# A list scheduler's picture of PSUM banks and of a cold TensorE, block norms applied behind the projection, and down sums of two hidden tiles

## The chip, the core and the metric

The kernel runs on one core of a Trainium2 chip. The metric is the device time of one execution in microseconds (us); the time before is the median of three runs, 3055.63 us (3053.68 to 3060.42). TensorE (PE) multiplies, VectorE (DVE), ScalarE (ACT) and GpSimd (POOL) do the rest, SyncE (SP) issues the DMAs.

## What is computed

One step of a hybrid decoder layer, for a prompt of 2048 tokens and eight single decode tokens that share the weights, in float32:

```python
y = parallel_mixer(rms_norm(x, norm_mix), ...)        # p = h @ w_in; a width-31 depthwise conv on a gated half,
x = x + y                                             # a gated DeltaNet of 4 heads on the other; then w_out
x = x + memory_attend(rms_norm(x, norm_mem_q), ...)   # 4 heads over 256 memory tokens
x = x + swiglu(rms_norm(x, norm_ffn), w_gate, w_up, w_down)   # 1024 -> 2816 -> 1024
y = rms_norm(x, norm_f)

def rms_norm(x, g, eps=1e-6):
    return x * rsqrt(mean(x * x, -1) + eps) * g
```

The outputs are the two y, the new convolution and DeltaNet states and the memory's keys and values.

## The kernel before

The prompt is cut into NB = 4 blocks of TB = 512 tokens; the features lie on the partitions, in KC = 8 tiles of 128. Float32 precision is reached by splitting every factor into a high and a low part and adding three products (`three`), so each product of a 128x128 tile is three matmuls (x3 in the rows). The split of x into the two parts is made by `split_ps`: ScalarE writes the high part, VectorE subtracts for the low one. Weights arrive as `raw` tiles and are split into NW = 6 tiles `w`, by ScalarE and then GpSimd or VectorE, for the first block that uses them; the FFN's split tiles are kept in DRAM (`sums`) and read from there by the later blocks.

Stages in the profiled run: to 860 us the mixer's projections for the pairs of blocks (0, 1) and (2, 3), products `hd` (q, k, v, z), `glua` and `glub` from the tiles `hT`, with the DeltaNet heads (`dn_front`, `dn_chain`: pk, pq, pqk, pu, pch, po) and the depthwise convolution on VectorE (`cacc`, 480 instructions) beside them; to 945 memory keys and values; to 1303 output projection (`rg`) and attention (`sc`) of blocks 0 and 1; the FFN of block 0 to 1680; then output and attention of block 2, FFN 1, the same of block 3, FFN 2 (with the eight decode columns) and FFN 3. An FFN has NF = 22 hidden tiles f; for each there are seven products fx, fy, fz of 12 matmuls of 256 columns, and the down sums `dn`, which are added to x (`x<-dn,x`).

`norm_in` (L1121) prepares blocks 1 to 3 in two passes over x: the first loads each of 8 tiles `xl`, squares it (`sqj`) and sums the squares, whose row factor goes through `pss`, `rs`, `dg` and `prs` (TensorE, VectorE, GpSimd) to `rsb`; the second loads `xl` again, multiplies it by gain and `rsb`, and splits it into `hT`. Block 0 already does it the other way: its `hT` carry only the gain, and `evac` (L1554) multiplies by `rsb` when a product leaves PSUM. `down` (L2675) sums GF = 4 hidden tiles in a PSUM bank before it adds to x: NG = 6 groups, the last of two; a group's eight output tiles are spread over the four following f.

PSUM has eight banks: three under the tag mm, three under s, one each under o and cv. Nothing is issued as written: each operation goes on a `Tape`, and `Tape.order` (L283) lists them anew. It runs a clock for each engine, takes from each engine's ready operations the one with the lowest key, and adds the estimated duration from `cost` (L176) and a latency. What an operation depends on is found by comparing boxes (`box`, L207), so that two uses of different parts of one PSUM bank are independent. The result is one fixed order for each engine. TensorE has one estimated price for each shape, whatever went before.

Of the kernel before, what the change touches and what calls it, by code (L numbers as in the profile page):

```python
# [14 lines left out]
P = 128  # L15
# [29 lines left out]

PAIRS = [(b, b + 1) for b in range(0, NB, 2)]
GF = 4
NG = -(-NF // GF)
# [11 lines left out]
HOLD = 2  # L60
RES = 5
# [85 lines left out]
class Tape:  # L147
# [28 lines left out]
    def cost(self, eng, op, args, kw, outs, ins):  # L176
# [16 lines left out]
        if eng == "act":  # L193
            ptr = len(ins) - 1
            return 0.834 * n + (50 if psum_in else 94) + 93 * ptr, False, SETS.get(kw.get("func"))
# [87 lines left out]
    def order(self):  # L283
# [49 lines left out]
        dma_at, port_at, table = 0.0, 0.0, None  # L333
# [15 lines left out]
        while len(done) < N:  # L349
# [18 lines left out]
            while av:  # L368
                k, n = heappop(av)
                new = [x for x in tiles[n] if x not in given]  # L370
# [7 lines left out]
                if stop is None:  # L378
                    if e == "dve" and self.ops[n][7][1] and port_at > t + 150 and not skipped:

                        other = [(k2, m) for k2, m in av if not self.ops[m][7][1] and all(x in given for x in tiles[m])]
# [45 lines left out]
            done.append(n)  # L427
            lat = self.LAT["dma" if e == "sp" else e]
# [144 lines left out]
def hybrid_step(ctx: ExitStack, tc: tile.TileContext, i: dict, o: list):  # L573
# [209 lines left out]
    def span_of(k, left):  # L783

        n = KC // min(GF, left)
        return range(k * n, (k + 1) * n)

    def group(g):
        return range(GF * g, min(GF * (g + 1), NF))

    def down_keys(g, ms=range(KC)):

        return [("w_down", "f", KC * g + (m if g < NG - 1 else m // 2), 0) for m in ms if g < NG - 1 or m % 2 == 0]

    def ffn_steps(b):
# [3 lines left out]
        for f in range(NF):  # L799
            if f and not early:  # L800
                steps.append(("Q1", f))
            g = f // GF - 1
            ms = span_of(f % GF, NF - GF * (g + 1))
            if g < 0 or g >= NG - hold:
                g = None
# [7 lines left out]
            if g is not None:  # L813
                steps.append(("down", g, ms[0]))
            steps.append(("P4", f))
            if g is not None:
                steps += [("down", g, m) for m in ms[1:]]
        if not hold and b != NB - 1:
            steps += [("down", NG - 1, m) for m in range(KC)]
# [11 lines left out]
    def ffn_plan(b):  # L831
        at = {}
        for st, f, *j in ffn_steps(b):
            if st == "down":
                plan.extend(down_keys(f, j))
# [30 lines left out]
    for b in range(NB):  # L866
# [4 lines left out]
        elif b + 1 < NB:  # L871
            for g in range(NG - HOLD, NG):
                plan.extend(down_keys(g))
    plan.extend(down_keys(NG - 1))
# [3 lines left out]
    class WS:  # L878
# [28 lines left out]
        def load(self):  # L907
# [9 lines left out]
            else:  # L917
                w, kind, a, b_ = what
                src = wsrc[w]
                if kind == "c":  # L920
                    dma(r, src[a, b_], fr)
                elif kind == "f":
                    dma(r, src[a], fr)
# [197 lines left out]
    def norm_in(b, res, go=1):  # L1121

        acc = None
        yield go
        for second in range(2):
            xs = []
            for k in range(KC):
                while len(xs) < min(k + 3, KC):
                    yield ("t2", 1 + RES)
                    xs.append(t2("xl"))  # L1130
                    dma(xs[-1], xT[len(xs) - 1, :, cols_of(b)])
                x = xs[k]
                yield x
                if second:
                    yield ("act", 1)
                    a = act("hT")
                    V.scalar_tensor_tensor(out=x, in0=x, scalar=vcol("norm_mix", k), in1=rsb, op0=ALU.mult, op1=ALU.mult)
                    split_ps(x, a[:, 0, :TB], a[:, 1, :TB])
                    drop(x)
                    res[k] = a  # L1140
                else:
                    yield ("t2", 1 + RES)
                    j = square(x)
                    drop(x)
                    if acc is None:
                        acc = j
                    else:
                        G.tensor_tensor(out=acc, in0=acc, in1=j, op=ALU.add)
                        drop(j)
                yield 1  # L1150
            if not second:
                rs = yield from rstd([acc], TB)
                rsb = yield from spread(rs, TB)
        drop(rsb)
        res["rsb"] = None
# [278 lines left out]
    def scalars(b, hT, res):  # L1434
# [8 lines left out]
        if hT["rsb"] is None:  # L1443
            A.activation(out=bdf, in_=pb_, func=AF.Copy)
        else:
            V.tensor_tensor(out=bdf, in0=pb_, in1=hT["rsb"][:16], op=ALU.mult)
# [107 lines left out]
    def evac(out, pts, hT, func=AF.Copy):  # L1554
# [3 lines left out]
        for pt, lo, hi in pts:  # L1558
            if hT["rsb"] is None:
                A.activation(out=out[:, lo:hi], in_=pt, func=func)  # L1560
                continue
# [77 lines left out]
    def dn_front(h, b, sc, prev, out):  # L1639
# [27 lines left out]
        for c in range(NT):  # L1667
            j = small("chj", [P, DK], dt=mybir.dt.bfloat16, bufs=1)
# [10 lines left out]
        for c in range(NT):  # L1679
            j = small("chj", [P, DK], dt=mybir.dt.bfloat16, bufs=1)  # L1680
# [30 lines left out]
        yield lambda: not inverting  # L1711
        inverting.append(1)
# [21 lines left out]
        inverting.pop()  # L1734
# [44 lines left out]
    def dn_chain(h, b, f, sc, prev, out):  # L1779
# [8 lines left out]
        for c in range(NT):  # L1788
# [21 lines left out]
            j = small("chj", [P, DK], dt=mybir.dt.bfloat16, bufs=1)  # L1810
# [56 lines left out]
    kv_done, act_keep, fronts, inverting = [], [0], [], []  # L1867
# [157 lines left out]
    def glub_then(k):  # L2025
        def then(b, pts, dp):
# [5 lines left out]
            if hTs[b]["rsb"] is not None:  # L2032
                G.tensor_tensor(out=sg, in0=sg, in1=hTs[b]["rsb"], op=ALU.mult)
# [21 lines left out]
    for pair in PAIRS:  # L2055
# [58 lines left out]
        for b in pair:  # L2114
            S.until(lambda: "beta" in scs_[b], "scalars")
            if hTs[b]["rsb"] is not None:
                drop(hTs[b]["rsb"])
# [478 lines left out]
    def ffn(b, op, go_on):  # L2596
# [76 lines left out]
        dwt = {}  # L2673

        def down(g, m):  # L2675
            fs = group(g)
            S.until(lambda: all(f in hact for f in fs), "ff")
            for key in down_keys(g, (m,)):
                dwt[0] = [ws.get(*key)]
            spans = [(0, w), (w, 2 * w)] if b == DEC_F else [(0, TB)]  # L2680
            pts = [pm("dn", (P, hi - lo)) for lo, hi in spans]
            for n_, f in enumerate(fs):
                at = n_ if g < NG - 1 else 2 * (m % 2) + n_
                three(pts, wk(dwt[0], 0, at), wk(dwt[0], 1, at), hact[f], spans, n_ == 0, n_ == len(fs) - 1)
                tick()
            if g < NG - 1 or m % 2:
                ws.free(1)
            if b == DEC_F:
                add_half(m, pts)
            else:  # L2690
                add_x(xs, m, [(pts[0], 0, TB)], None)
            if g == NG - 1:
                fin.add(m)
            if m == KC - 1:
                drop(*[hact.pop(f) for f in fs])

        def rest():
            for g in range(NG - HOLD, NG):
                for m in range(KC):
                    down(g, m)  # L2700
# [3 lines left out]
        def last():  # L2704
            fs = (NF - 2, NF - 1)
            S.until(lambda: all(f in hact for f in fs), "ff")
            wts = [ws.get(*key) for key in down_keys(NG - 1)]
# [83 lines left out]
def lay_out(inp):  # L2791
# [33 lines left out]
    full = NF // GF * GF  # L2825
    wd = inp["w_down"][0].reshape(NF, P, KC, P)
    main = wd[:full].reshape(NG - 1, GF, P, KC, P).transpose(0, 3, 2, 1, 4).reshape(-1, P, TB)
    end = wd[full:].reshape(2, P, KC // 2, 2, P).transpose(2, 1, 3, 0, 4).reshape(-1, P, TB)
    out["w_down"] = np.concatenate([main, end])
# [35 lines left out]
```

## Time and profile before

| | |
|---|---|
| median of three runs | 3055.63 us |
| profiled execution | 3056.0 us |
| its span | 3054.3 us |
| granted TensorE clock, mean | 0.988 |
| PE busy | 2958.2 us (97%) |
| DVE busy | 1971.5 us (65%) |
| POOL busy | 1380.7 us (45%) |
| ACT busy | 1325.6 us (43%) |

All instructions carry the line of one helper (L450, L469 in the changed kernel), so they are told apart by their tiles: `pss<-ones,sqj` writes pss and reads ones and sqj. [...]

### The profile page before, as it was taken

To read this page: it belongs to the slowest core of one execution; us is meant where nothing else is said; L and a number is where in the kernel's file an instruction comes from. 1 tells how busy PE (TensorE), PEld (TensorE's weight loads), DVE (VectorE), ACT (ScalarE), POOL (GpSimd) and SP (SyncE) were. 2 spreads that over 40 slices of the span, in tenths; PEclk is the share of its full clock that TensorE was granted. 3 is DMA by queue.
4 is the path that set the end of the run, shared out by engine and by line. 5 is a ranking of instruction groups with operands and counts; after the bars stand their busy time and mean duration, and the time that the engine had idled before them with its cause. 6 is when DMAs were issued, how large, how long until landed. Compare 5 with 4: busy or idle time off the path is not lost.

```text
span 3054.3 us, 52803 instructions
## 1 busy us (share of the span) xinstructions
PE 2958.2 (97%) x18950; PEld 2625.0 (86%) x18950; DVE 1971.5 (65%) x3946; ACT 1325.6 (43%) x2695; POOL 1380.7 (45%) x1228
## 2 busy tenths in 40 slices
PE   8999989999999999989999999999999999999998
PEld 6898867888888878789988779988878999999997
DVE  7857888888986876687678885423576333553334
ACT  6643337543565343545455354333444332433333
POOL 3433333432446455678877204355512443444444
PEclk9999989999999999999999999999999999999999
DMA  6443334543676442277667748766534766676663
GB/s 232 153 131 101 116 114 142 160 147 96 189 255 188 134 140 80 89 245 265 233 251 262 238 136 283 253 227 232 180 117 145 241 215 218 207 244 221 220 221 109
DMA packets 358631, 567.24 MB, mean 186 GB/s; under 512 B 56832, under 2 KB 155072, under 8 KB 358352
## 3 DMA queue, kind: packets, MB, share of 16 engines
q1 hardware_dynamic: 358368, 563.86, 55.9%
q8 instruction: 150, 2.46, 0.3%
q14 instruction: 113, 0.93, 0.1%
HBM read 455.68 MB, written 108.64 MB: 185 GB/s over the span
## 4 chain that ended last, share of the span: by engine, by line
PE 72%; DVE 7%; DMA 4%; ACT 1%; issue 1%; POOL 1%; SPq 0%; POOLq 0%; DVEq 0%; ACTq 0%
PE dn L450 16%; PE fy L450 12%; PE rg L450 9%; PE fz L450 8%; PE fx L450 8%; PE sc L450 5%; PE hd L450 4%; DVE cacc L450 2%; PE pu L450 2%; PE glub L450 1%; PE glua L450 1%; DVE bit L450 1%; PE pch L450 1%; DMA Tm<-zt 1%; DMA w<-sums 1%
## 5 line engine op out<-in xcount | busy, mean ns | idle before, releaser
L450 POOL TENSOR_TENSOR w<-raw,w 128x512 fp32r<-128x512 f32 x683 | 931.4, 1369 | 955.0 <-ACT w L450 866.7
L450 ACT ACTIVATE w<-raw 128x512 fp32r<-128x512 f32 x912 | 568.3, 631 | 942.9 <-PE dn L450 231.9
L450 PE MATMUL dn<-ff,w 128*128 128x512 f32 (+2 forms) x2688 | 518.2, 346 | 0.8 <-ACT ffs L450 0.8
L450 PEld LDWEIGHTS dn<-ff,w 128*128 128x128 f32 x2688 | 421.5, 188 | 58.8 <-ACT ffs L450 1.0
L450 PE MATMUL fy<-op,w 128*128 128x256 f32 (+1 forms) x3168 | 426.8, 283 | 0.5 <-DMA w<-sums 0.5
L450 PEld LDWEIGHTS fy<-op,w 128*128 128x128 f32 x3168 | 403.0, 189 | 8.5 <-issue 1.4
L450 PE MATMUL hd<-hT,w 128*128 128x512 f32 (+2 forms) x1920 | 399.6, 359 | 8.8 <-ACT w L450 6.6
L450 DVE SCALAR_TENSOR_TENSOR cacc<-cu,cw,cacc 128x512 f32<-128x512 f32 x480 | 358.7, 747 | 16.2 <-ACT cacc L450 11.0
L450 PEld LDWEIGHTS hd<-hT,w 128*128 128x128 f32 x1920 | 306.4, 191 | 52.6 <-ACT w L450 6.8
L450 PE MATMUL fz<-op,w 128*128 128x256 f32 (+1 forms) x2112 | 286.4, 282 | 4.2 <-DMA w<-sums 2.1
L450 PE MATMUL fx<-op,w 128*128 128x256 f32 (+1 forms) x2112 | 285.7, 283 | 2.9 <-DVE op L450 1.6
L450 PEld LDWEIGHTS fx<-op,w 128*128 128x128 f32 x2112 | 270.9, 189 | 12.8 <-DVE op L450 2.1
L450 PEld LDWEIGHTS fz<-op,w 128*128 128x128 f32 x2112 | 265.9, 189 | 8.9 <-issue 3.9
L450 DVE TENSOR_TENSOR w<-raw,w 128x512 fp32r<-128x512 f32 x229 | 217.8, 959 | 69.6 <-ACT w L450 67.3
L450 DVE TENSOR_TENSOR x<-dn,x 128x512 f32<-128x512 f32 (+1 forms) x248 | 139.8, 567 | 174.9 <-PE dn L450 172.5
L450 POOL TENSOR_TENSOR sqj<-sqj,sqj 128x512 f32<-128x512 f32 (+1 forms) x98 | 130.2, 1328 | 266.9 <-ACT sqj L450 264.7
L450 PE MATMUL sc<-w,hT 128*128 128x512 f32 x768 | 193.2, 404 | 3.0 <-DVE w L450 1.8
L450 PE MATMUL rg<-catS,w 128*128 128x512 f32 (+2 forms) x960 | 191.9, 355 | 1.9 <-DVE x L450 1.9
L450 PE MATMUL rg<-pT,w 128*128 128x512 f32 x768 | 190.6, 399 | 0.3
L450 PEld LDWEIGHTS rg<-catS,w 128*128 128x128 f32 x960 | 153.9, 189 | 26.9 <-DVE x L450 2.2
L450 PEld LDWEIGHTS sc<-w,hT 128*128 128x128 f32 x768 | 142.7, 191 | 37.6 <-ACT pr L450 3.1
L450 PEld LDWEIGHTS rg<-pT,w 128*128 128x128 f32 x768 | 141.4, 188 | 33.6 <-ACT pr L450 3.0
(381 smaller groups left out, 4036.3 us busy)
## 6 DMA issues: line engine op xcount, KB each, us to landing
w<-sums SPq DMA_DIRECT2D x264, 512.0 KB, 4.4
raw<-in_w_gate_dram SPq DMA_DIRECT2D x176, 256.0 KB, 3.4
sums<-w SPq DMA_DIRECT2D x88, 512.0 KB, 3.2
raw<-in_w_down_dram SPq DMA_DIRECT2D x176, 256.0 KB, 3.4
raw<-in_w_up_dram SPq DMA_DIRECT2D x110, 256.0 KB, 2.7
raw<-in_w_in_dram SPq DMA_DIRECT2D x96, 256.0 KB, 2.8
raw<-in_w_out_dram SPq DMA_DIRECT2D x64, 256.0 KB, 3.2
raw<-wk SPq DMA_DIRECT2D x64, 256.0 KB, 2.6
```

The source lines that it names most:

```text
L450: fn(*args, **kw)
```

## The change

1. The planner: a PSUM tile has one box, so a bank is one piece in the dependencies. `bank_at` also keeps an engine off a bank until another engine's last access to it is over. TensorE's estimates count 1.9 times for 3.4 us after it has had a pause of over 1.8 us. A ScalarE instruction that also accumulates costs 92 ns more.
2. `norm_in` makes `hT` and the squares in one pass, with the gain only; `rsb` is applied in `evac` for every block. That takes away 24 loads of `xl` and 24 VectorE scalings, and ScalarE's direct evacuations of blocks 1 to 3; VectorE gets those evacuations: `raw<-hd,rsb` of 512 columns 12 to 36 and of 256 columns 0 to 24, zs and sg each 4 to 12 and 0 to 8; GpSimd gets `sg<-sg,rsb` 4 to 16. In all VectorE has 4280 instructions for 3946, GpSimd 1245 for 1228, SP's DMAs are 1842 for 1866, and TensorE's matmuls stay the same in number.
3. Down groups of two: NG = 11, HOLD = 3. At an even f from 2 to 18 all eight output tiles of group f/2 - 1 are done one behind the other (four weight tiles of two outputs each), at an odd f none but at the last. `x<-dn,x` of 512 columns go from 136 to 256, of 256 columns from 112 to 192; matmuls and weight tiles stay the same in number.
4. The DeltaNet inversions no longer wait for each other (`inverting` is gone), and the junk tile `chj` of the squared norms has four buffers for one.

```diff
 def box(self, a):
+        if a.name in self.psum:
+            return 0, 0, 0, 0
...
+        def bank_at(n, e):
+
+            return max([bank[x][1] + self.LAT[bank[x][0]][e] for x in banks[n] if x in bank and bank[x][0] != e], default=0.0)
...
                 k, n = heappop(av)
+                at_ = bank_at(n, e)
+                if at_ > t:
+                    ready[n] = at_
+                    push(n)
+                    n = None
+                    continue
...
+            if e == "pe" and s > clock[e] + 1800 and s > 5000:
+                slow = s + 3400
+            if e == "pe" and s < slow:
+                ns *= 1.9
...
     def norm_in(b, res, go=1):
...
+        for k in range(KC):
+            while len(xs) < min(k + 4, KC):
+                yield ("t2", 1 + RES)
+                xs.append(t2("xl"))
+                dma(xs[-1], xT[len(xs) - 1, :, cols_of(b)])
+            x = xs[k]
+            yield x
+            yield ("act", 1)
+            a = act("hT")
+            split_ps(x, a[:, 0, :TB], a[:, 1, :TB], scale=vcol("norm_mix", k))
+            res[k] = a
...
+        res["rs"] = yield from rstd([acc], TB)
+        res["rsb"] = yield from spread(res["rs"], TB)
...
         for pt, lo, hi in pts:
-            if hT["rsb"] is None:
-                A.activation(out=out[:, lo:hi], in_=pt, func=func)
-                continue
             V.tensor_tensor(out=out[:, lo:hi], in0=pt, in1=hT["rsb"][:, lo:hi], op=ALU.mult)
...
-            g = f // GF - 1
-            ms = span_of(f % GF, NF - GF * (g + 1))
-            if g < 0 or g >= NG - hold:
+            g = NG - 2 if f == NF - 1 else f // 2 - 1 if f % 2 == 0 and 0 < f < NF - 2 else None
+            if g is not None and g >= NG - hold:
                 g = None
...
-            j = small("chj", [P, DK], dt=mybir.dt.bfloat16, bufs=1)
+            j = small("chj", [P, DK], dt=mybir.dt.bfloat16, bufs=4)
...
-        yield lambda: not inverting
-        inverting.append(1)
```

The order that comes out differs at many places. Three of them, all on TensorE:

At the start, before: what stands between block 0's first products and the first product of block 1 (hd_304, hd_305, in the 256 and 264 columns that block 1 and the decode tokens make); prs spreads a row factor, pbd is the small product for beta and decay.

```order
L450 MATMUL prs_279<-dg_273,ones 128x512
L450 MATMUL pbd_329<-hT_235,wbd 16x512 x2
L450 MATMUL pbd_329<-hT_237,wbd 16x512
L450 MATMUL pbd_280<-wbd,hd_mix 8x16
L450 MATMUL pbd_329<-hT_237,wbd 16x512
L450 MATMUL pbd_329<-hT_239,wbd 16x512 x2
L450 MATMUL pbd_329<-hT_241,wbd 16x512 x2
L450 MATMUL pbd_280<-wbd,hd_mix 8x16 x15
L450 MATMUL pss_275<-ones,sqj_251 128x1 x4
L450 MATMUL pbt_333<-ident,bdf_330 128x16 x4
L450 MATMUL prs_287<-dg_281,ones 128x512
L450 MATMUL hd_304<-hT_291,w_219 128x256
```

After, from the same dnb (the decode tokens' norm) on; block 1's first product is now hd_295:

```order
L469 MATMUL dnb_286<-tbd_278,ones 128x8
L469 MATMUL hd_295<-hT_252,w_219 128x256 x3
L469 MATMUL hd_295<-hT_255,w_219 128x256
L469 MATMUL pbd_321<-hT_225,wbd 16x512 x2
L469 MATMUL pbd_321<-hT_227,wbd 16x512 x2
L469 MATMUL hd_295<-hT_255,w_219 128x256 x2
L469 MATMUL hd_295<-hT_258,w_219 128x256
L469 MATMUL pbd_321<-hT_229,wbd 16x512 x2
L469 MATMUL pbd_321<-hT_231,wbd 16x512 x2
L469 MATMUL pbd_321<-hT_235,wbd 16x512 x2
L469 MATMUL hd_295<-hT_258,w_219 128x256 x2
L469 MATMUL hd_295<-hT_261,w_219 128x256
```

Block 1's product moved from behind both prs to the row behind dnb; the first prs, prs_287, now stands four rows further down.

Near 404 us, before: chain work of block 1, block 3's row factor (prs_1019), and then block 3's first product (hd_985<-hT_1028):

```order
L450 MATMUL peb_1099<-dtmp_962,ones 128x64
L450 MATMUL pch_1020<-chr_1021,W_872 128x128
L450 MATMUL lnb_1022<-tbd_1013,ones 128x8
L450 MATMUL prs_1019<-dg_1014,ones 128x512
L450 MATMUL po_989<-chv_1033,at_724 128x128
L450 MATMUL pch_1020<-chv_1033,kd_722 128x128
L450 MATMUL pbd_1101<-hT_904,wbd 16x512 x2
L450 MATMUL pbd_1101<-hT_906,wbd 16x512 x2
L450 MATMUL pbd_1101<-hT_912,wbd 16x512 x2
L450 MATMUL pbd_1101<-hT_916,wbd 16x512 x2
L450 MATMUL pbd_1101<-hT_924,wbd 16x512
L450 MATMUL hd_985<-hT_1028,w_928 128x512
```

After: block 2's last product of the three (hd_974), block 3's first (hd_980) right behind it, with chain work between its parts:

```order
L469 MATMUL hd_974<-hT_882,w_918 128x512 x3
L469 MATMUL hd_974<-hT_929,w_918 128x512 x3
L469 MATMUL hd_974<-hT_931,w_918 128x512 x3
L469 MATMUL hd_980<-hT_965,w_885 128x512 x3
L469 MATMUL pm_981<-cd_927,ones 128x8 x4
L469 MATMUL hd_980<-hT_970,w_885 128x512 x3
L469 MATMUL po_960<-S_121,rb_716 128x128
L469 MATMUL po_960<-chv_975,at_719 128x128
L469 MATMUL pch_962<-chv_975,kd_717 128x128
L469 MATMUL hd_980<-hT_977,w_885 128x512 x3
L469 MATMUL lnc_994<-ones,cd_770_967 8x1 x4
L469 MATMUL pch_998<-S_983,kT_711 128x128
```

Block 3's product moved ahead of its row factor; hd_980, hd_1029 and hd_1039, 24 rows' worth of x3, stand ahead of prs_1026 but for the last x3.

Near 1750 us, before: attention scores sc of block 2 with the transposes psc of the decode tokens' scores scs between them:

```order
L450 MATMUL sc_3738<-w_3760,hT_3744 128x512 x3
L450 MATMUL sc_3739<-w_3760,hT_3744 128x512 x3
L450 MATMUL sc_3740<-w_3760,hT_3744 128x512 x3
L450 MATMUL sc_3754<-w_3760,hT_3744 128x512 x3
L450 MATMUL psc_3799<-ident,scs_3546 32x128
L450 MATMUL sc_3805<-w_3765,hT_3692 128x512 x3
L450 MATMUL sc_3805<-w_3770,hT_3694 128x512
L450 MATMUL psc_3799<-ident,scs_3546 32x128
L450 MATMUL sc_3805<-w_3770,hT_3694 128x512 x2
L450 MATMUL sc_3805<-w_3775,hT_3696 128x512 x2
L450 MATMUL sc_3796<-w_3765,hT_3692 128x512 x3
```

After: the last score products, the first products behind them, and psc:

```order
L469 MATMUL sc_3813<-w_3817,hT_3750 128x512 x3
L469 MATMUL sc_3814<-w_3817,hT_3750 128x512 x3
L469 MATMUL rg_3839<-pT_3819,w_3821 128x512 x3
L469 MATMUL rg_3848<-pT_3819,w_3821 128x512 x3
L469 MATMUL rg_3846<-pT_3819,w_3821 128x512 x3
L469 MATMUL rg_3839<-pT_3823,w_3829 128x512 x2
L469 MATMUL rg_3847<-pT_3819,w_3821 128x512 x3
L469 MATMUL rg_3839<-pT_3823,w_3829 128x512
L469 MATMUL rg_3846<-pT_3823,w_3829 128x512 x3
L469 MATMUL rg_3847<-pT_3823,w_3829 128x512 x3
L469 MATMUL rg_3848<-pT_3823,w_3829 128x512 x3
L469 MATMUL psc_3855<-ident,scs_3565 32x128 x2
```

Both psc moved from the beginning of the second group of scores to behind that group and the first rg.

## Rows read from the trace of the kernel before

**Rows 1.** The page's part 1: busy us, share of the span, instructions.
```profile
PE 2958.2 (97%) x18950; PEld 2625.0 (86%) x18950; DVE 1971.5 (65%) x3946; ACT 1325.6 (43%) x2695; POOL 1380.7 (45%) x1228
```

**Rows 2.** Windows: stretch, length, busy us (instructions) by engine, clock, DMA.
```profile
core 0: us, PE busy (x) PEld busy (x) DVE busy (x) ACT busy (x) POOL busy (x), PEclk, DMA share, GB/s
450.00:850.00 400.00, 391.15 (x2149) 322.77 (x2150) 346.96 (x790) 202.06 (x437) 155.94 (x184) 1.00 0.48 147
28.00:46.00 18.00, 11.42 (x58) 6.48 (x57) 12.84 (x38) 5.42 (x9) 8.36 (x11) 0.78 0.90 310
404.00:428.00 24.00, 17.39 (x74) 12.90 (x73) 17.74 (x45) 8.03 (x16) 7.07 (x12) 0.57 0.39 122
1743.00:1765.00 22.00, 16.08 (x59) 11.92 (x58) 18.31 (x48) 9.55 (x25) 0.00 (x0) 0.77 0.43 134
1350.00:1700.00 350.00, 348.14 (x2296) 314.64 (x2295) 261.64 (x341) 170.29 (x314) 269.36 (x188) 1.00 0.72 254
1850.00:1900.00 50.00, 50.00 (x387) 47.80 (x386) 25.56 (x42) 19.08 (x36) 20.59 (x14) 1.00 0.84 289
2700.00:2750.00 50.00, 48.90 (x396) 47.68 (x397) 25.48 (x43) 17.12 (x34) 21.45 (x15) 1.00 0.87 305
```

**Rows 3.** Timeline of TensorE at the start: start, length, instruction, [idle before, releaser].
```profile
31.76 2.07 PE L450 MATMUL prs<-dg,ones 128*128 128x512 f32 x2 [2.43 <-DVE dg L450]
...
39.30 0.39 PE L450 MATMUL pbt<-ident,bdf 16*128 16x16 f32 x4 [1.84 <-DVE bdf L450]
...
43.12 1.24 PE L450 MATMUL hd<-hT,w 128*128 128x256 f32 x4 [2.19 <-ACT hT L450]
```

**Rows 4.** Timeline of TensorE from 404 to 428.
```profile
414.96 1.87 PE L450 MATMUL pss<-ones,sqj 128*128 128x1 f32 x8 [2.75 <-POOL sqj L450]
...
421.57 2.04 PE L450 MATMUL prs<-dg,ones 128*128 128x512 f32 x2 [1.10 <-DVE dg L450]
...
427.74 0.62 PE L450 MATMUL hd<-hT,w 128*128 128x512 f32 x2
```

**Rows 5.** Timeline of TensorE from 1745 to 1762.
```profile
1744.67 3.88 PE L450 MATMUL sc<-w,hT 128*128 128x512 f32 x16
...
1753.74 0.39 PE L450 MATMUL psc<-ident,scs 128*32 128x128 f32 x1 [4.09 <-DVE scs L450]
...
1757.25 4.94 PE L450 MATMUL sc<-w,hT 128*128 128x512 f32 x11 [1.84 <-DVE w L450]
```

**Rows 6.** Waits of TensorE over the span: us, times, longest.
```profile
PE pu L450 <- DMA Tm<-zt: 6.6, 6, 2.5
...
PE pq L450 <- ACT chj L450: 5.2, 6, 1.8
...
PE pod L450 <- ACT chj L450: 3.2, 2, 1.7
...
PE ppt L450 <- ACT chj L450: 2.3, 1, 2.3
```

**Rows 7.** Groups of instructions, shapes apart: count | busy us, mean ns | idle before.
```profile
L450 DVE SCALAR_TENSOR_TENSOR cacc<-cu,cw,cacc 128x512 f32<-128x512 f32 x480 | 358.7, 747 | 16.2 <-ACT cacc L450 11.0
L450 DVE TENSOR_TENSOR w<-raw,w 128x512 fp32r<-128x512 f32 x229 | 217.8, 959 | 69.6 <-ACT w L450 67.3 <-DMA raw<-in_w_up_dram 0.5 <-DMA raw<-in_w_out_dram 0.4
L450 DVE TENSOR_TENSOR x<-dn,x 128x512 f32<-128x512 f32 x136 | 93.7, 689 | 128.9 <-PE dn L450 128.1
L450 DVE TENSOR_TENSOR x<-dn,x 128x256 f32<-128x256 f32 x112 | 46.1, 419 | 46.0 <-PE dn L450 44.3
L450 DVE SCALAR_TENSOR_TENSOR xl<-xl,vcol,rsb 128x512 f32<-128x512 f32 x24 | 17.0, 740 | 2.0 <-DMA xl<-in_xT_dram 1.1 <-ACT rsb L450 0.9
...
L450 DVE TENSOR_TENSOR raw<-hd,rsb 128x512 f32<-128x512 f32 x12 | 8.1, 684 | 3.2 <-ACT rsb L450 2.0 <-PE hd L450 1.2
...
L450 POOL TENSOR_TENSOR sg<-sg,rsb 128x512 f32<-128x512 f32 x4 | 5.2, 1291 | 14.1 <-ACT sg L450 14.1
```

**Rows 8.** Timeline of TensorE in FFN 3.
```profile
2717.95 0.59 PE L450 MATMUL fz<-op,w 128*128 128x256 f32 x3 [1.10 <-DMA w<-sums]
```

More of the change, by code (lines that the diff above doesn't have):

```diff
@@ L58 @@
 DEC_F = 2
-HOLD = 2
+HOLD = 3
 RES = 5
@@ L332, in order @@
         clock = dict.fromkeys(engines, 0.0)
-        dma_at, port_at, table = 0.0, 0.0, None
+        dma_at, port_at, table, slow = 0.0, 0.0, None, 0.0
+        banks = [[x for x in ts if x in self.psum] for ts in tiles]
+        bank = {}
+        def bank_at(n, e):
+            return max([bank[x][1] + self.LAT[bank[x][0]][e] for x in banks[n] if x in bank and bank[x][0] != e], default=0.0)
         start, end, ends = [0.0] * N, [0.0] * N, {}
@@ L379, in order @@
                     if e == "dve" and self.ops[n][7][1] and port_at > t + 150 and not skipped:
-                        other = [(k2, m) for k2, m in av if not self.ops[m][7][1] and all(x in given for x in tiles[m])]
+                        other = [(k2, m) for k2, m in av if not self.ops[m][7][1] and all(x in given for x in tiles[m]) and bank_at(m, e) <= t]
                         if other:
@@ L427, in order @@
             done.append(n)
+            for x in banks[n]:
+                bank[x] = e, max(fin, bank[x][1]) if x in bank and bank[x][0] == e else fin
             lat = self.LAT["dma" if e == "sp" else e]
@@ L1121, in norm_in @@
     def norm_in(b, res, go=1):
+        xs = []
         acc = None
         yield go
[L1125 to L1155, printed above, removed]
+        for k in range(KC):
[9 more added lines that the diff above has]
+            res[k] = a
+            yield ("t2", 1 + RES)
+            j = square(x)
+            drop(x)
+            if acc is None:
+                acc = j
+            else:
+                G.tensor_tensor(out=acc, in0=acc, in1=j, op=ALU.add)
+                drop(j)
+            yield 1
+        res["rs"] = yield from rstd([acc], TB)
+        res["rsb"] = yield from spread(res["rs"], TB)
     def norm_mem(res):
@@ L1442, in scalars @@
         bdf = t2("bdf", (16, TB))
-        if hT["rsb"] is None:
-            A.activation(out=bdf, in_=pb_, func=AF.Copy)
-        else:
-            V.tensor_tensor(out=bdf, in0=pb_, in1=hT["rsb"][:16], op=ALU.mult)
+        V.tensor_tensor(out=bdf, in0=pb_, in1=hT["rsb"][:16], op=ALU.mult)
         yield bdf
@@ L2031, in then @@
             evac(sg, pts, hTs[b], AF.Sigmoid)
-            if hTs[b]["rsb"] is not None:
-                G.tensor_tensor(out=sg, in0=sg, in1=hTs[b]["rsb"], op=ALU.mult)
+            G.tensor_tensor(out=sg, in0=sg, in1=hTs[b]["rsb"], op=ALU.mult)
         return then
@@ L2115, in hybrid_step @@
             S.until(lambda: "beta" in scs_[b], "scalars")
-            if hTs[b]["rsb"] is not None:
-                drop(hTs[b]["rsb"])
+            drop(hTs[b]["rsb"])
     dma(o[3], halo)
@@ L2698, in rest @@
             for g in range(NG - HOLD, NG):
-                for m in range(KC):
-                    down(g, m)
+                for j in range(KC // 2):
+                    down(g, j)
             if b == DEC_F:
```

83 lines of the change are left out of this document (33 added, 50 removed).

## Prediction

> **What bounds the kernel now.** I read the page's busy times first, then the windows, the waits of TensorE, the timeline of the stretches that stood out, and last the groups of instructions. TensorE is busy for 2958.2 of 3054.3 us [rows 1], 97%, so this kernel can gain only what TensorE loses: some 96 us of idle time, and the time in which its clock is granted at the lower of its two levels. VectorE (65%), GpSimd and ScalarE (under half) are not bounds on the mean. The windows say where the loss is [rows 2]. 50 us of FFN products (1850 to 1900) have no idle time at a granted clock of 1.00, and the whole FFN of block 0 (1350 to 1700) lacks 1.9 of 350 us. The mixer between 450 and 850 lacks 8.9 of 400, with VectorE busy for 347 of the 400. Three short stretches lose far more for their length: 28 to 46, 404 to 428 and 1743 to 1765, with clocks of 0.78, 0.57 and 0.77. [...]
>
> **The change, part by part.** The sum is made against the profiled execution, 3056.0 us, which is 0.4 us above the median of the three runs, 3055.63.
>
> A, the start. Before, block 1's input is loaded twice: first for the squares, then, once its norm is known, for the scaled copies from which the products are made. TensorE therefore waits for the norm, 2.43 us at 31.76 (dg), then 1.84 at 39.30 and 2.19 at 43.12, where block 1's first product at last begins [rows 3]. Now the copies are made from the raw input on its first pass, and the row factor is applied when a product leaves PSUM. The order puts block 1's first product right behind the dnb that ends block 0's, with pbd, prs and the other small products between its parts, instead of behind prs. Bound: idle 6.6 + 0.22 x 18 = 4.0, so 10.5 us. I take 9: the work that fills the stretch (12 matmuls of 256 and 12 of 264 columns, some 3 us, before the second half of the copies) does not quite cover the 5 us of waits for dg, so something stays. Low end 6.
>
> B, block 3's norm at 404. TensorE waits 2.75 us for the sum of squares at 414.96, 1.10 for dg at 421.57, and the first product of block 3 stands at 427.74 [rows 4]; in between it does fragments of the chain at half clock. In the new order block 3's first product, its second and all but the last of its third (8 + 8 + 7 groups of x3) stand ahead of prs: 69 matmuls of 512 columns. At 0.233 us apart (16 such matmuls of sc take 3.88 us of which the last is 0.39 [rows 5]: 3.49/15) that is 16.1 us of dense work where there were fragments. Bound: idle 6.6 + 0.43 x 24 = 10.3, so 16.9 us. I take 14. Low end 8: the three products fill the three banks of their tag and hold them until block 3's row factor is there, so a norm that is late moves the wait behind the third product.
>
> C, the decode scores at 1743. The two transposes psc wait 4.09 us for VectorE's scs, and the next scores 1.84 for w, which VectorE makes behind it [rows 5]. Now both psc stand behind all scores of the pair and behind the first rg products. Bound: 5.9 idle + 0.23 x 22 = 5.1, so 11 us. I take 7, the waits and 1 of the clock; low end 3, if another VectorE operand is late next.
>
> D, banks. "Waits for chj" are TensorE waiting for a bank that ScalarE still reads (a square, then an accumulator read): pq 5.2 us, pod 3.2, ppt 2.3 [rows 6], and five smaller ones of 0.6 to 1.0, 14.4 us in all. The planner before thought a part of the bank free at once. Now it knows the bank is one piece and that the accumulator costs more, so it puts other work there. I take half, 7, with 0 and 12 as ends. The six waits of pu for the Tm transfer (6.6 us) are not touched by banks; letting several inversions run at once moves them by 2 either way, so nothing.
>
> E, VectorE in the mixer. Blocks 1 to 3 lose 24 scalings of xl (740 ns), and gain 24 raw of 512 columns (684), 24 raw of 256 (taken as 419, the half-size x<-dn), and for zs and sg together 16 of either size. That is 24 x 0.684 + 24 x 0.419 + 16 x 0.685 + 16 x 0.419 - 24 x 0.740 = 16.4 + 10.1 + 11.0 + 6.7 - 17.8 = +26 us, with bdf and the STT form of hT +3: about 30 us [rows 7]. Against it the order moves depthwise taps (cacc, 747 ns) out of this part: 313 instead of 360 of the 480 stand ahead of the first attention-output add, -35 us. The net is -5 us, on an engine that is 87% busy in 450 to 850 while TensorE loses 8.9 us. But the new operations stand between a product and its bank, the taps did not. I take a loss of 2, between a gain of 4 and a loss of 8 (8.9 us of idle time nearly doubled).
>
> F, FFN of block 0. Down groups of two instead of four mean 11 instead of 6 sums for each of the 8 column tiles of a block. In block 0 that is some 24 more adds x<-dn at 689 ns, 17 us, and the taps that were moved (438 instead of 470 done at the first ffu) another 24; with the last chain step VectorE gets 55 us more in this stage. It had 88 us spare (350 - 262). TensorE lost 1.9 us there; with the spare down to 33 I scale by 88/33 to 5, a loss of 3, and take 5 with the three-bank tag turning over twice as often. Ends: a gain of 2 (all that is lost there) and a loss of 15 (the slices after 1600, in which VectorE has already least to spare, overflow).
>
> G, FFN of blocks 1 to 3. There VectorE is at half load and the extra adds cost nothing. What is new is the run of weights: 13 products with no down sum between them, then eight sums in a row on four tiles. Product-only stretches exist before: 1850 to 1900 has 50.00 of 50 at 289 GB/s, 2700 to 2750 48.90 with one wait of 1.10 us for a weight tile at 2717.95 [rows 2, 8]. I take 2, two such waits more; ends 0 and 10.
>
> Sum: 9 + 14 + 7 + 7 - 2 - 5 - 2 = 28 us, so 3056.0 - 28 = **3028 us**.
>
> [...] The rows show a VectorE add with one PSUM operand at 689 ns in the mean, and the split w<-raw,w of the same size, with two SBUF operands, at 959 [rows 7]. [...]
>
> **The rivals.**
> 1. Weight tiles come late in the long runs, and it ends slower. There are 10 such runs in a block, 40 in all. At the one wait that the trace shows, 1.10 us each, that is 44 us in place of G's 2: 3028 - 2 + 44 = 3070 us. It decides from (28 + 2)/40 = 0.75 us a run. For it: 2717.95 is exactly such a wait, and the four tiles of a group are now wanted one behind the other. Against it: 1850 to 1900 is longer than a run and has no wait. Chance 0.11.
> 2. The gaps only move. The order is fixed on the planner's estimates; the three banks hold block 3's products until its row factor comes, and other chain steps wait in front of them in the queue. If A, B and C bring half (15), D nothing, and the losses stay (9), it is -6: 3050 us, at the edge of what can be told from no change. That the planner's new rules don't do what they say belongs here: the chj waits then stay at 14. Chance 0.15.
> 3. VectorE becomes the bound in block 0's FFN and in the mixer: F 15, E 8, G 2 against 37: 3044 us. For it: VectorE's load there goes from 262 to about 317 of 350, unevenly. Against it: adds wait for TensorE now, for the most part, and can slide. Chance 0.09.
> 4. All goes well: 10.5 + 16.9 + 11 + 12 with no losses is 50: 3006 us. Chance 0.07.
> 5. The clock. The 50 us of products in 1850 to 1900 change banks every 12 matmuls of 256 columns and hold 1.00 [rows 2]; the new down sums change them every 6 of 512, which takes as long. If instead the clock fell in them as far as in 28 to 46 (0.78), about 490 us of down matmuls (2112, in units of 512 columns, at 0.233) would take 490 x (1/0.78 - 1) = 138 us more, 3166 us. [...] Chance 0.01.
>
> **How the numbers follow.** The forecast (3012 to 3044) has 0.57, the rivals 0.11, 0.15, 0.09, 0.07 and 0.01. 0.2% of 3055.6 is 6 us, about what a measurement of this kernel can tell from no change. Faster by more: the forecast, rivals 3 and 4 and a third of rival 2, 0.78. The same: most of the rest of rival 2 and the milder half of rival 1, 0.10. Slower: the rest, 0.12. Best ends together (4) give 3006; the low end of the range is there. At the top, the low ends of A to D (6 + 8 + 3 + 0 = 17) less the losses' upper ends (8 + 15 + 10 = 33) are +16, not all likely together; 3060 leaves most of rival 1 and rival 5 out, near 0.12, and a little below the low end.
>
> **What would show it.** Right: 28 to 46 and 404 to 428 with TensorE dense and the clock at 1.00; no psc wait near 1750; chj waits near 7 us; VectorE about 300 of 350 in block 0's FFN with TensorE idle there under 10 us. Wrong: waits of fx, fy, fz or dn for w<-sums that add up to over 20 us (rival 1); waits of products for raw<-hd,rsb or for rsb in the mixer (rival 2); waits of FFN products for x<-dn, or a longer FFN of block 0 (rival 3); lower clock in the down runs (rival 5).

## The result and the profile after

The changed kernel takes 3013.76 us (median of four runs, 3007.98 to 3015.80) against 3056.39 us in the same comparison: ratio 0.9856 (a kernel's time over that of the kernel before, run beside it), interval 0.9839 to 0.9874, or 44 us less. All gains and losses of the experiments below are differences of such ratios, times 3056 us. Its profiled execution is the fastest of the four, 3007.98 us, so the two traces differ by 48 us and the medians by 43.

The page's part 1 after, to be held against [rows 1]:

```profile
PE 2935.5 (98%) x18950; PEld 2610.7 (87%) x18950; DVE 2082.1 (69%) x4280; ACT 1303.0 (43%) x2651; POOL 1405.4 (47%) x1245
```

VectorE works 111 us more, TensorE 23 us less for the same 18950 matmuls: less of its work is done at the lower clock. Read in windows of 1 us, the granted clock of both traces is 1.00 or 0.50, with 23 windows before and 11 after in between and none below 0.50: two levels, the lower half of the upper. Score products sc of 512 columns start 0.233 us apart at 1.00 (from 1744.67 on, before) and 0.43 us apart at 0.50 (1759.97, 1760.40, 1760.83). The mean granted clock went from 0.988 to 0.994. What the windows lack to 1.00 adds up to 36.7 us before and 19.2 after; at 0.50 that is about 73 us at the lower level before and 38 after. TensorE's idle time went from 96.1 us (3054.3 - 2958.2) to 70.6. So of the 48 us about 25 are waits; the lower clock that went with them is, by the estimate, up to 18 of the 23 that are left (half of the 35 us less at the lower level).

The windows of stretches in [rows 2], after (block 2's scores, at 1743 before, stand at 1697 now; 1300 to 1325 is new here):

```profile
28.00:46.00 18.00, 18.00 (x133) 14.24 (x134) 15.92 (x41) 5.63 (x9) 7.85 (x12) 1.00 0.56 206
404.00:428.00 24.00, 24.00 (x126) 16.52 (x125) 23.39 (x49) 13.25 (x20) 11.79 (x16) 1.00 0.35 108
1300.00:1325.00 25.00, 10.87 (x68) 10.08 (x69) 24.65 (x57) 5.59 (x11) 14.07 (x12) 0.73 0.53 176
1697.00:1719.00 22.00, 20.42 (x93) 16.29 (x92) 20.41 (x46) 11.12 (x26) 0.00 (x0) 1.00 0.62 206
2700.00:2750.00 50.00, 50.00 (x347) 46.40 (x346) 21.83 (x38) 15.94 (x30) 23.29 (x18) 1.00 0.68 223
```

The start and block 3's norm are dense, and the scores lose 1.6 of 22 us, all at a clock of 1.00. From 1300 to 1325 TensorE is busy for 10.9 of 25 us with VectorE full. The FFN of block 0 starts 69 us earlier now, so 1350 to 1700 would no longer be the same work. These are the same stages, before and then after: first memory, output and attention of blocks 0 and 1, then the FFN of block 0 from its first fx to its last.

```profile
860.00:1303.00 443.00, 423.17 (x2453) 360.63 (x2452) 331.25 (x675) 212.63 (x478) 233.47 (x204) 0.99 0.45 143
820.00:1234.00 414.00, 403.43 (x2378) 344.19 (x2377) 306.62 (x650) 202.29 (x465) 212.78 (x192) 1.00 0.47 147
```

```profile
1303.00:1652.00 349.00, 338.46 (x2324) 309.47 (x2323) 264.69 (x355) 172.08 (x324) 272.41 (x189) 0.99 0.72 255
1234.00:1605.00 371.00, 350.98 (x2455) 320.72 (x2454) 296.76 (x460) 184.35 (x364) 295.48 (x214) 0.98 0.71 243
```

In the first TensorE's idle time falls from 19.8 to 10.6 us; in the second it grows from 10.5 to 20.0, and TensorE does 131 matmuls more there, so the two stages exchange work too. Some of the waits of TensorE, after:

```profile
PE fx L469 <- ACT ffu L469: 11.0, 2, 10.5
PE hd L469 <- ACT w L469: 6.2, 2, 6.0
...
PE pu L469 <- DMA Tm<-zt: 2.9, 2, 2.4
...
PE fz L469 <- DMA w<-sums: 1.7, 1, 1.7
PE fy L469 <- DMA w<-sums: 1.6, 3, 1.1
...
PE prs L469 <- DVE dg L469: 1.6, 1, 1.6
```

No row for chj is left, where [rows 6] had 14.4 us in all, and none for psc. The timeline of TensorE at the start shows how [rows 3] closed up:

```profile
31.53 1.55 PE L469 MATMUL pbd<-hT,wbd 128*16 128x512 f32 x6
32.91 1.02 PE L469 MATMUL prs<-dg,ones 128*128 128x512 f32 x2
33.37 1.49 PE L469 MATMUL pbd<-hT,wbd 128*16 128x512 f32 x4
34.77 1.02 PE L469 MATMUL pss<-ones,sqj 128*128 128x1 f32 x8
35.66 0.74 PE L469 MATMUL hd<-hT,w 128*128 128x264 f32 x4
```

The 10.5 us wait is read on two engines. VectorE's groups from 1275 to 1318, and the timeline of ScalarE and TensorE at its end:

```profile
L469 DVE SCALAR_TENSOR_TENSOR cacc<-cu,cw,cacc 128x512 f32<-128x512 f32 x19 | 14.0, 738 | 0.0
L469 DVE TENSOR_TENSOR w<-raw,w 128x512 fp32r<-128x512 f32 x10 | 8.2, 828 | 0.0
L469 DVE TENSOR_TENSOR x<-dn,x 128x512 f32<-128x512 f32 x8 | 5.4, 676 | 0.2 <-PE dn L469 0.2
```

```profile
1317.40 0.63 ACT L469 ACTIVATE ff<-ffu 128x512 fp32r<-128x512 f32 x1 [7.06 <-DVE ffu L469]
...
1317.94 0.36 ACT L469 ACTIVATE ffu<-fx 128x256 f32<-128x256 f32 x1
...
1318.36 2.93 PE L469 MATMUL fx<-op,w 128*128 128x256 f32 x12 [10.51 <-ACT ffu L469]
```

Here ffu, ffs and ff are tiles between the products fx, fy, fz and a finished hidden tile. TensorE wants a bank that ScalarE has yet to empty (`ffu<-fx`); ScalarE stands behind `ff<-ffu`, which waits for a VectorE product (ffu); and VectorE, without a pause in these 43 us, is at depthwise taps, weight splits and the last DeltaNet inversion (bit), whose last big operation starts at 1314 here and at 1134 before.

### The profile page after: what moved, and what is told of

Same layout as the page of the kernel before. It is cut to its first block, busy times and chain, and to the rows that moved or that the text cites. A ratio compares the mean times of both kernels' runs of the same rounds, so it can differ in the third digit from the quotient of the medians.

```text
span 3006.1 us, 53090 instructions
## 1 busy us (share of the span) xinstructions
PE 2935.5 (98%) x18950; PEld 2610.7 (87%) x18950; DVE 2082.1 (69%) x4280; ACT 1303.0 (43%) x2651; POOL 1405.4 (47%) x1245
## 4 chain that ended last, share of the span: by engine, by line
PE 82%; DVE 10%; DMA 4%; issue 2%; ACT 1%; POOL 1%; SPq 0%; DVEq 0%; POOLq 0%; ACTq 0%
PE dn L469 16%; PE fy L469 12%; PE rg L469 10%; PE hd L469 9%; PE fx L469 8%; PE fz L469 8%; PE sc L469 5%; DVE cacc L469 3%; PE pu L469 2%; PE glua L469 2%; PE glub L469 2%; DVE bit L469 1%; PE pch L469 1%; DVE acc L469 1%; DMA w<-sums 1%
## 5 line engine op out<-in xcount | busy, mean ns | idle before, releaser
L469 PE MATMUL hd<-hT,w 128*128 128x512 f32 (+2 forms) x1920 | 406.7, 360 | 6.2 <-ACT w L469 6.2
L469 DVE TENSOR_TENSOR x<-dn,x 128x512 f32<-128x512 f32 (+1 forms) x448 | 254.0, 571 | 131.1 <-PE dn L469 128.1
L469 DVE TENSOR_TENSOR w<-raw,w 128x512 fp32r<-128x512 f32 x223 | 196.1, 886 | 66.8 <-ACT w L469 66.1
L469 DVE TENSOR_TENSOR ffu<-fy,ffu 128x256 f32<-128x256 f32 (+1 forms) x176 | 74.4, 423 | 176.8 <-PE fy L469 176.6
L469 PE MATMUL rg<-catS,w 128*128 128x512 f32 (+1 forms) x960 | 192.1, 354 | 0.8 <-DVE x L469 0.8
```

Of the source, the lines that this page charges most:

```text
L469: fn(*args, **kw)
```

## Where the loss lies, stage by stage

For each matmul I take the time to the next one's start, less the median of that time for the same tile and shape over all traces here, and add this up by stages of equal matmul work, so that kernels whose stages lie at other times can be compared. The sums are estimates from single traces; for before and after they give 47 us of the 48. Names e1 to e8 are the experiments below (e4 is not in the table).

| loss in us | before | after | e1 | e2 | e3 | e5 | e6 | e7 | e8 |
|---|---|---|---|---|---|---|---|---|---|
| start | 16 | 4 | 10 | 15 | 13 | 9 | 4 | 4 | 4 |
| rest of pair (0, 1) | 11 | 5 | 15 | 3 | 11 | 11 | 5 | 5 | 9 |
| block 3's norm | 22 | 5 | 8 | 14 | 19 | 11 | 5 | 5 | 24 |
| rest of pair (2, 3) | 19 | 17 | 21 | 18 | 23 | 18 | 14 | 19 | 26 |
| memory, output and attention 0, 1 | 44 | 26 | 42 | 35 | 40 | 42 | 27 | 48 | 56 |
| FFN 0, first part | 13 | 22 | 23 | 14 | 12 | 26 | 31 | 8 | 27 |
| all behind | 26 | 25 | 26 | 35 | 37 | 28 | 36 | 38 | 28 |

## The experiments

The theory ahead of them: each part's gain lies at its own places, so the parts can be taken apart. The rivals: only the planner's picture of banks makes the freed stretches useful; or every new order merely shuffles the gaps.

**e1, the norms alone.** The kernel before with the one-pass `norm_in` and the row factor in `evac` for all blocks.

```diff
-        for second in range(2):
...
+            split_ps(x, a[:, 0, :TB], a[:, 1, :TB], scale=vcol("norm_mix", k))
...
+        res["rsb"] = yield from spread(res["rs"], TB)
```

> The kernel before with only the one-pass norms of blocks 1 to 3 (part 2). Theory, the gains lie at separate places: this part alone removes the losses at the start and at block 3's norm near 404 us (in the comparison of the two traces 10 and 24 us), so 3056 - 34 = 3022 us, 3012 to 3032, with 28 to 46 and the stretch near 404 dense at clock 1.00, and the waits of TensorE for chj still over 10 us. Rival, the planner's bank rule is what makes the freed stretches dense: then block 3's products stop at a held bank, near 400 us at least 10 us of TensorE's idle time stay, and the time is 3040 or more.

Measured: 3050.43 us, ratio 0.9969 (0.9957 to 0.9981), 10 us less instead of 34. Both stretches are dense, as the theory had it, but the gain is given back. Windows:

```profile
28.00:46.00 18.00, 18.00 (x134) 14.27 (x133) 16.96 (x41) 6.17 (x9) 8.32 (x13) 1.00 0.65 222
404.00:428.00 24.00, 23.19 (x128) 18.91 (x127) 22.35 (x45) 12.43 (x26) 17.46 (x15) 1.00 0.50 148
1300.00:1350.00 50.00, 37.39 (x253) 34.36 (x252) 45.37 (x73) 16.86 (x32) 35.01 (x29) 0.83 0.59 197
```

In the table it gains 20 us at the start and at block 3's norm, and, against that, loses 10 in the first part of FFN 0 (its waits there are fy for ffs, 10.6 us, and dn for ffs, 3.7) and 6 in the rest of the mixer. VectorE got work and TensorE got there sooner: a part of the wait moved to where the two meet next. So the rival's mechanism (held banks near 404) is not it, and neither is the theory's sum.

**e2, the planner alone.**

```diff
+        if a.name in self.psum:
+            return 0, 0, 0, 0
...
+                at_ = bank_at(n, e)
...
+                ns *= 1.9
```

> The kernel before with only the planner's part 1 (bank as one piece, half rate after a pause, price of accumulation). Theory: it removes waits for chj (14 us before) and the psc waits (6 us with the scores behind them) and leaves the losses at the start and near 404, so 3056 - 18 = 3038 us, 3030 to 3046. Rival, each new order only shuffles the gaps: chj waits fall, but others come in their place, 3050 to 3062.

Measured: 3043.19 us, ratio 0.9946 (0.9927 to 0.9965), 17 us less, as expected in size, but not in its places. The chj waits fall from 14.4 to 0.7 us, and block 3's norm, which was to stay as it was, loses 8 us less (22 to 14). But psc stays, and the last row of the table is 9 us worse:

```profile
PE psc L471 <- DVE scs L471: 4.1, 1, 4.1
...
PE pod L471 <- ACT chj L471: 0.7, 2, 0.4
```

**e3, the groups of two alone.**

```diff
-GF = 4
-NG = -(-NF // GF)
+NG = NF // 2
...
-HOLD = 2
+HOLD = 3
```

> The kernel before with only the down groups of two (part 3). Theory: no gain and little loss, 3052 to 3066 us, with FFN 1 to 3 as dense as before and at most 5 us more of loss in block 0's FFN, where VectorE has more adds. Rival, groups of two give TensorE product work earlier and save on their own: under 3048 us.

Measured: 3064.67 us, ratio 1.0022 (1.0010 to 1.0034), 7 us more: the theory's case. The extra adds of block 0 cost nothing that the table shows (12 for 13 in its first part); the loss is behind it. The psc wait is gone here, with the planner and the norms as before.

**e4, the change with the old planner.** All of the change but part 1.

```diff
-        if a.name in self.psum:
-            return 0, 0, 0, 0
...
-                at_ = bank_at(n, e)
...
-                ns *= 1.9
```

> The changed kernel with the planner's part 1 taken back (parts 2, 3 and 4 stay). Theory: the waits for chj return (12 us or more) and psc's or others with them, 3014 + 16 = 3030 us, 3022 to 3040, with the start and block 3's norm as dense as in the changed kernel. Rival: without the bank rule the norm's gain goes too, 3040 or more.

Measured: 3052.49 us, ratio 0.9981 (0.9971 to 0.9990). The time is the rival's: of the change's 44 us only 6 are left. The places are the theory's, for the start and block 3's norm stay nearly as dense as in the change:

```profile
28.00:46.00 18.00, 18.00 (x133) 14.11 (x134) 17.44 (x42) 6.20 (x10) 9.30 (x13) 1.00 0.70 227
404.00:428.00 24.00, 22.55 (x129) 18.39 (x128) 23.22 (x44) 9.53 (x21) 18.09 (x16) 1.00 0.48 141
```

So the norms' gain is kept there and given back elsewhere. The chj waits are back:

```profile
PE fx L448 <- ACT ffu L448: 10.7, 2, 10.5
PE pq L448 <- ACT chj L448: 9.1, 7, 3.8
...
PE pk L448 <- ACT chj L448: 5.8, 10, 1.5
```

Three smaller rows make it 16.6 us, more than before, although chj now has four buffers. TensorE neither reads nor writes chj, so I read them not as waits for the buffer, but for the bank that the squares read.

**e5, the change with banks in parts.** Of part 1 only the bank rule is taken out.

```diff
-        if a.name in self.psum:
-            return 0, 0, 0, 0
...
-                at_ = bank_at(n, e)
+                at_ = 0.0
```

> The changed kernel with the bank rule taken out of the planner (a PSUM tile's parts are independent again and an engine's access does not keep others off); the half rate after a pause and the price of accumulation stay. Theory: the bank rule is nearly all that the planner's part brings, so 3044 to 3056 us, near the 3052 of the kernel with the whole part taken back, with waits for chj of 10 us or more. Rival, the price of accumulation alone (92 ns on each square) moves TensorE's work enough: 3030 us or less.

Measured: 3046.17 us, ratio 0.9974 (0.9965 to 0.9984). The bank rule alone carries 36 of the 38 us by which e4 falls short of the change (0.9974 and 0.9981 against 0.9856). The chj waits are 15.3 us. The table shows some 17 us lost against the change in the mixer's four rows and 16 in memory, output and attention. How much of these 33 us hangs on the chj waits, by the clock and by the work behind them, is not shown.

**e6, the change with groups of four.** Part 3 taken back.

```diff
-NG = NF // 2
+GF = 4
+NG = -(-NF // GF)
...
-HOLD = 3
+HOLD = 2
```

> The changed kernel with the down groups of four and HOLD 2 as before (parts 1, 2 and 4 stay). Theory: groups of two cost a little in block 0's FFN and bring nothing, so 3003 to 3016 us, and the wait of fx of about 10 us near 1318 stays, since it comes from VectorE's backlog of depthwise taps and inversions and not from the adds. Rival, the adds of groups of two make that wait: then it falls below 4 us. Second rival, groups of two bring something in company: 3022 or more.

Measured: 3025.74 us, ratio 0.9909 (0.9895 to 0.9924): 16 us worse than the change, the second rival. The fx wait is not due to the adds, as the theory had it; with about half as many of them it is no shorter (11.8 us). And psc is back:

```profile
PE fx L471 <- ACT ffu L471: 12.0, 2, 11.8
...
PE fz L471 <- DVE ffu L471: 5.5, 1, 5.5
...
PE psc L471 <- DVE scs L471: 3.3, 1, 3.3
```

**e7, the change with one inversion at a time.**

```diff
+        yield lambda: not inverting
+        inverting.append(1)
...
+        inverting.pop()
```

> The changed kernel with one DeltaNet inversion at a time again. Theory: no more than a reshuffle, 3008 to 3022 us; the waits of pu for Tm go back from 3 us to some 6. Rival, inversions at once are what fills VectorE near 1300 to 1318: then the wait of fx there falls below 4 us and the time to 3006.

Measured: 3028.36 us, ratio 0.9916 (0.9900 to 0.9933), 18 us worse. Both readings are half true: the wait of fx at FFN 0 falls to 3.9 us (8 us of loss in that stage for 22), but memory, output and attention lose 22 us more (48, with the bank rule in place), and the last two inversions now run at 1321 and 1477, inside the FFN.

**e8, the taps first.** One edit in the planner's keys, on top of the change.

```diff
                 key[n] = min([n + LATER, *after])
+                if self.ops[n][0] == "dve" and any("cacc" in t for t in tiles[n]):
+                    key[n] = n - 1500
```

> The changed kernel with the planner's key of the depthwise taps lowered by 1500, which puts 360 of the 480 taps ahead of the first output-projection add (313 in the changed kernel) and all 480 ahead of the first down add (456). Theory: the 10.5 us that TensorE waits for fx near 1318 is VectorE's backlog, part of it taps moved there; with them gone it is below 4 us, and the time is 3004 to 3012. Rival, the taps then stand before other VectorE work of the mixer, which pays as much there: 3012 to 3025 with over 5 us more loss before 890 us.

Measured: 3074.93 us, ratio 1.0073 (1.0058 to 1.0088), 66 us worse than the change and above both ranges. The 10.5 us wait is gone (no wait of fx over 2.7 us), yet the first part of FFN 0 loses more than in the change (27 for 22), and the taps cost far more elsewhere. TensorE at block 3's norm, and VectorE there:

```profile
418.78 0.79 PE L471 MATMUL po<-chv,at 128*128 128x128 f32 x2 [6.02 <-DVE chv L471]
```

```profile
416.81 0.73 DVE L471 SCALAR_TENSOR_TENSOR cacc<-cu,cw,cacc 128x512 f32<-128x512 f32 x1
417.47 0.99 DVE L471 TENSOR_TENSOR bit<-biq,w 32x512 f32<-32x512 f32 x1
418.39 0.33 DVE L471 TENSOR_SCALAR chv<-pch,brk 128x128 f32<-128x128 f32 x1
```

A chain step of 0.33 us (chv) stands behind taps and inversion steps, and TensorE waits 6 us for it. The late taps of the change are thus the better choice of the two.

**e9, no norms in company.** The planner, groups of two and chj, but the old norms and the lock (without the norms, the planner finds no order with inversions at once). It is held against e7.

```diff
+        for second in range(2):
...
-            split_ps(x, a[:, 0, :TB], a[:, 1, :TB], scale=vcol("norm_mix", k))
```

> The changed kernel without the one-pass norms, and with one inversion at a time (without the norms, inversions at once leave the planner no order): the planner's part, groups of two and the four chj buffers. To be held against e7, the same with the norms, 3028 us. Theory, the norms bring over 15 us once the banks are planned, against 8 alone: 3044 to 3060 us, with 10 us or more of the loss back at the start and near 404. Rival, the parts add up: 3028 + 8 = 3036, 3030 to 3042.

Measured: 3041.86 us, ratio 0.9940 (0.9924 to 0.9956) against 0.9916 of e7: 7 us, about the 10 of e1. The loss at the start and near 404 is back, as the theory had it:

```profile
28.00:46.00 18.00, 10.28 (x48) 4.88 (x47) 11.77 (x37) 6.60 (x11) 11.62 (x10) 0.70 0.93 317
404.00:428.00 24.00, 18.90 (x72) 14.45 (x71) 17.70 (x38) 11.72 (x24) 10.64 (x15) 0.72 0.58 182
```

But in the sum the rival holds by the ratios, with intervals that overlap. So no gain of the norms from the planner shows; as far as these intervals tell, they bring 7 to 10 us net either way.

**e10, no half rate.** `slow = 0.0` in place of `slow = s + 3400`.

```diff
-                slow = s + 3400
+                slow = 0.0
```

> The changed kernel without the planner's half rate after a pause; banks and accumulation as in the change. The order on TensorE is the same up to the beginning of block 0's FFN. Theory: this piece is worth little, 3008 to 3022 us, with the wait of fx near 1318 as before it. Rival, it carries a part of the gain in the FFN and the attention of block 2: 3024 or more.

Measured: 3016.29 us, ratio 0.9850 (0.9828 to 0.9871), the same as the change, with the wait of fx at 10.5 us as before. The planner's half rate is worth nothing that can be measured here.

**e11 and e12, VectorE priced higher.** A price 10% and 20% higher for VectorE operations with two tensors from SBUF, on top of the change; the work is the same (the lines are e11's, e12 has 1.2).

```diff
-            return 68 + (61 if ptr else 0) + n * (...), big > 1, None
+            t = 68 + (61 if ptr else 0) + n * (...)
+            return t * (1.1 if big > 1 else 1.0), big > 1, None
```

> The changed kernel with VectorE operations that read two tensors from SBUF priced 10% higher in the planner. In the trace of the changed kernel the split w<-raw,w takes 886 ns in the mean against a price of 601. Theory: the 10.5 us wait near 1318 is a misjudged VectorE, and with a higher price TensorE gets other work there, the wait falls under 5 us and the time to 3002 to 3011. Rival: another order with gaps of its own, 3013 to 3035.

> The same with 20%. Theory: as with 10%, 3000 to 3011 us and the wait near 1318 under 5 us. Rival: another order with gaps of its own, 3013 to 3035.

Measured: 3020.60 us, ratio 0.9870 (0.9854 to 0.9886), and 3030.78 us, 0.9902 (0.9880 to 0.9925). The fx wait falls to 6.5 and 6.3 us, not below 5, and other gaps come. The rival in both, and a measure of it: these edits, which change nothing but the order, move this kernel by 4 and 14 us. e8 is such an edit too, a coarser one, and moved it by 66. No version tried is clearly faster than the change.

## Why the prediction was right, point by point

The forecast was 28 us less, 3028 us; it is 43 less, 3014. Direction and range hold; the sum was short by a third, and 3014 lies near the low end of the forecast's own 3012 to 3044. That it came so near is in part luck: the terms below missed both ways, and two parts of the change (the inversions, the groups of two) have in company a worth that the sum did not have.

- **A and B, the norms.** Forecast 9 and 14, and in the table 12 and 17 between before and after. The mechanism is as told: 28 to 46 and 404 to 428 are dense at clock 1.00, in e1 too (to 0.8 us) and in e4 (to 1.5), and not in e9 without the norms. The bounds of A to C add (1 - clock) x length to the idle time as an upper end; the products sc, 0.43 us apart at 0.50 for 0.233 at 1.00, come near that. What the steps left out is that a stretch freed on TensorE is paid for in part elsewhere, in e1 above all in block 0's FFN, where TensorE waits for VectorE's and ScalarE's ffs: e1 is 10 us faster for 20 us of loss gone in these two stages.
- **C, the psc waits.** Forecast 7, by the order alone and with no part named as the cause. The wait is gone in all ten kernels with groups of two, and it is there in the four without (before, e1, e2, e6: 3.3 to 4.2 us), whatever the planner's rules. So it is an effect of part 3. Since it goes in e3 too, it does not tell why groups of two cost 7 us alone and are worth 16 in company. Block 2's output and attention, from the last fx of block 0 to the first of block 1, lose 11 us before and 6 after, by sums like the table's: 5 us, not 7.
- **D, the banks.** The term that was mis-sized. Forecast 7, "half" of 14.4 us of chj waits; they went entirely, and the bank rule is worth 36 us in company (e5) and the planner 17 alone (e2). The step counted the waits themselves and nothing else that the planner's new picture moves. The largest single difference of the table, at memory, output and attention (44 to 26), is mostly not these waits: only 2.9 of the 14.4 us of chj lay there before. Nor is it the bank rule alone, for e7 has the rule and loses 48 there. That stage and the first part of FFN 0 have to be read together, since they exchange work: 57 us before, 48 after, 49 with the planner alone (e2), 68 without the bank rule (e5), 56 with the inversions locked (e7), 58 with groups of four (e6).
- **The inversions.** Step D put running several at once at nothing, as 2 us either way in the waits of pu. Those fell by 3.7 us (6.6 to 2.9), and taking this part back costs 18 us in company (e7).
- **E, VectorE in the mixer.** Forecast a loss of 2, found a gain of 2 in the rest of pair (2, 3) and of 6 in the rest of pair (0, 1), where D's chj waits lay too, so the table does not tell E apart there. e1, with the norms and the old planner, loses 6 in these two rows, within E's end of 8.
- **F, FFN of block 0.** Forecast a loss of 5, found 9, within its end of 15. The sign that was to show it failed: TensorE's idle time there is 20 us, not under 10, though VectorE's work grew by 32 us (265 to 297) and not by the step's 55. Of the causes that the step named, the adds are not it: there are 72 in this stage for 36, so 36 more and not the 24 that the step counted, and e3, which has them, shows no loss, while e6 has 36 and loses more. The moved taps are in it: VectorE's backlog at the long wait is 19 taps, beside weight splits and the last inversion, which the step left out. e1 loses 10 in that stage with the norms alone; with norms and one inversion at a time in company (e7) the loss is below that of before. Of rival 3's signs one came, a longer FFN of block 0 (349 to 371 us), in part by the work that it took over.
- **G and rival 1.** Waits for w<-sums are 3.3 us in all after, against 44 for rival 1. The runs of 13 products are fed. But the losses that F and G set for groups of two (7 us together) hold for these groups alone (e3); in company they are worth 16 (e6), and no step had that. Rival 5 falls with the clock of 1.00 in 2700 to 2750 and in every window of 1 us from 1323 to 2994; no run shows a clock that falls with changes of banks.
- **Rival 2** (the gaps only move) did not come true for the change, and did without the bank rule: e4 and e5 end at 3052 and 3046, near the 3050 that it named.

What stays open is where the bank rule's 36 us go beyond the chj waits, and why the parts are worth more together than apart: alone they give -10, -17 and +7 us, 20 in sum (the unlocked inversions were not tried alone), together 44. The bank rule is the only one whose value in company (36) is far beyond what the two small reorderings do (e11, e12: 4 and 14). It is itself an edit of the order alone, as is e8 with its 66 us, so size is not the proof. That it does what it says is read from the chj waits: at most 0.7 us in all nine kernels with the rule (the change, e2, e6 to e12), 11 to 17 in all five without it. The 16 and 18 us of e6 and e7 are just beyond 14, and may in part be luck of the order.

## What to carry to other kernels

Where a program sets the order of a kernel, an error in its picture of a resource, here banks that were thought divisible, can cost more than the sum of the waits that name it (here 36 us against 15 of chj waits in e5): repair it before the work around it. A stall removed on a full engine can be given back at its next meeting with a second engine (here half of e1's 20 us): look where that engine's backlog comes due. And before a part is credited with its difference, measure how far an edit moves the time that only reshuffles the order.

## What the runs showed of the hardware

Where pauses of TensorE were taken away, time at its lower clock went with them: idle time fell by 25 us and the time at the lower level by some 35 (73 and 38 us, an estimate from windows of 1 us), which at half rate is up to 18 us of work. The start and block 3's norm show it in one place each: clocks of 0.78 and 0.57 with 6.6 us of idle time before, 1.00 with none after. In both, and at block 2's scores, the idle time came first: TensorE stood from 29.33, 404.85 and 1749.65 us, and the first windows under 1.00 begin at 31, 406 and 1751. The forecast had counted this for three stretches only. The waits that the trace names by a junk tile (chj) are read as waits for a PSUM bank under two engines: four buffers for the tile did not remove them (16.6 us in e4), the planner's rule on banks did, but for 0.7 us, with one buffer too (e2). One of them, before: TensorE's transpose into pq began at 100.20 us after 1.77 us of idle time, 0.05 us behind the end of ScalarE's accumulator read for pq (99.95 + 0.20).
